# Cached stick-breaking keys loaded into the ring's key tiles and turned by VectorE, and cross-attention's key tiles requested a step ahead

## The chip, the cores and the metric

The kernel runs on one core of a Trainium2 chip. TensorE (PE), VectorE (DVE), ScalarE (ACT) and GpSimd (POOL) each run their instructions in order and wait for each other by semaphores; SyncE (SP) issues all of the kernel's DMAs here, also in order. The metric is the time of one execution in microseconds on the device; lower is better. The time before is 1880.95 us, the median of three runs (1879.8, 1880.95, 1893.64).

## The reference

One step of a hybrid encoder: 1024 prompt rows of one stream and 16 new rows of each of 8 running streams, 1152 rows in all, width 1024, fp32. The parts that the change touches are the attention of the 8 running streams over cached keys, and the cross-attention of these streams over cached memory:

```python
def mixers(u, p, past):
    proj = jnp.einsum('bnd,de->bne', u, p['w_in'])
    sq, sk, sv, fq, fk, fv, fg, z, xbc, dt = split_last(proj, IN_SIZES)
    ...
        sb_k = jnp.concatenate([past['sb_k'].astype(sk.dtype), sk], axis=1)
        sb_v = jnp.concatenate([past['sb_v'].astype(sv.dtype), sv], axis=1)
        sb_o = sb_attend(sq, sb_k, sb_v, qpos, kpos)
    ...
def sb_attend(q, k, v, q_pos, k_pos):
    z = jnp.einsum('bqhd,bkhd->bhqk', q, k).astype(jnp.float32) * (HEAD_DIM ** -0.5)
    valid = k_pos[None, :] < q_pos[:, None]
    log_keep = jnp.where(valid, jax.nn.log_sigmoid(-z), 0.0)
    after = lax.cumsum(log_keep, axis=3, reverse=True) - log_keep
    w = jnp.where(valid, jnp.exp(jax.nn.log_sigmoid(z) + after), 0.0)
    return jnp.einsum('bhqk,bkhd->bqhd', w, v.astype(jnp.float32)).astype(q.dtype)

def cross_attend(u, mk, mv, wq, wo):
    q = jnp.einsum('bnd,de->bne', u, wq).reshape(b, n, X_HEADS, X_HEAD_DIM)
    s = jnp.einsum('bnhd,bmhd->bhnm', q, mk.astype(q.dtype)).astype(jnp.float32) * (X_HEAD_DIM ** -0.5)
    pr = jax.nn.softmax(s, axis=-1)
    o = jnp.einsum('bhnm,bmhd->bnhd', pr, mv.astype(jnp.float32)).astype(u.dtype)
    return jnp.einsum('bne,ed->bnd', o.reshape(b, n, D_MODEL), wo)
```

The cached stick-breaking keys are 8 streams x 1024 positions x 4 heads x 64 (8.4 MB), the cached memory keys 8 streams x 256 positions x 4 heads x 256 (8.4 MB). Beside these the layer has a FoX attention with the same cache layout, an SSD scan, the projections and a SwiGLU feed-forward.

## The kernel before

Products in fp32 precision are made as three reduced-precision products of split operands (`mm3`, L338 to L340): every weight is loaded raw, copied to a high part (ACT) and subtracted to a low part (POOL). A *ring* of buffers holds them: four raw tiles (tag `wr`, `raw_t`, 128x528) and three pairs of split tiles (tags `wh` and `wl`, 128x1056). `w_unit` (L313 on; its load is L324) fills them for one unit of a projection.

The program runs in stages: memory projection and norms (to about 75 us), the projection `w_in` woven with stick-breaking attention (m = 0), then FoX (m = 1) and the SSD scan (about 150 to 700 us), the output projection, cross-attention (about 805 to 1060), and the feed-forward to the end. `pipeline` takes one unit of attention at a time and after each lets a filler go one step, which is a piece of the projection. The order on each engine is then set by a scheduler from a timeline that it simulates, with priorities (`hp`) that the code gives; the code's order is its start.

**Cached keys of the running streams.** `decode_units(0)` puts four pairs of streams into the attention pipeline, as units 3, 7, 11 and 15 (`AT0`). `rows(p)` makes the scores of a pair in two halves of 512 positions (`emit_past`). Each half needs two key tiles, one a stream, that have head dimension on partitions and positions along the row. `load_k(hf, b2)` makes one: two DMAs of 256 KB bring the keys as they lie (2 KB runs, L892) into two raw tiles of the ring, eight PE transposes turn 128x128 blocks into PSUM (L898), and two ACT copies of 128x512 (L900) bring them into the tile `kf`, which takes a slot of `wh` or `wl`. `quads` (L883) then multiplies 32 columns of queries with 512 positions, four products side by side on PE. A raw tile is free for the next weight load once its transposes are done, and a `kf` once its products are.

For m = 0 that is 16 calls of `load_k`: 32 DMAs, 128 transposes and 32 copies; for FoX (m = 1) the same again, which the change leaves.

**Cross-attention.** For each head, `x_query(hd)` projects the queries of all rows (`psd<-act,wh` on PE, six steps, two pairs of the ring), and `both(hd - 1)` runs the previous head's attention between its steps: `x_prompt` for the prompt rows and `x_sample` for the running streams, two steps of it after each step of the projection (`weave`, L435). In `x_sample` (L1571) a head's cached keys come in four tiles (pool `ws`), each by four DMAs of 32 partitions x 16 runs of 256 B (L1603) and one DVE transpose in blocks of 32x32 in place (L1607). `products` (L1592) multiplies after every second tile. Head 3 has no next projection: its `x_sample` and `x_prompt` run beside `loads()`, which brings the outputs of heads 0 to 2 back (`act<-osc`, L1392; first six blocks of 128x4x384 with heads 0 and 1), and the start of the next projection, `wo_x` (`psd<-wh,act` on PE), which reads them.

## Time and profile before

| | |
|---|---|
| median of 3 runs | 1880.95 us (1879.8 to 1893.64) |
| profiled execution | 1883.03 us, of it 1881.3 in the span |
| busy PE, DVE, ACT, POOL | 97%, 48%, 42%, 33% of the span |
| mean granted PE clock | 0.989 of full speed |
| L898, key transposes of m = 0 (128) | 18.5 us busy on PE |
| L900, copies of them (32) | 17.9 us busy on ACT |
| L1607, DVE transposes of memory keys (16) | 19.9 us busy on DVE |
| DMA | 296.6 MB in 312,028 packets, 113,340 of them under 512 B |

A row of a group names the source line, the engine, the operation, the tile written and the tiles read, the shapes, the count, busy time in us, mean ns of one, and the idle time of the engine just before them with what ended it. In the chain and the timelines the first number is the start in us, the second the length; `SPq` is SP issuing a DMA, and `[2.46 <-DMA act<-osc]` is 2.46 us of idle time that this DMA ended. Matmuls are pipelined, so that their busy times overlap; the price of one is read from the distance of starts or from the chain.

### The profile page before, as it was taken

To read this page: it belongs to the slowest core of one execution; us is meant where nothing else is said; L and a number is where in the kernel's file an instruction comes from. 1 tells how busy PE (TensorE), PEld (TensorE's weight loads), DVE (VectorE), ACT (ScalarE), POOL (GpSimd) and SP (SyncE) were. 2 spreads that over 40 slices of the span, in tenths; PEclk is the share of its full clock that TensorE was granted. 3 is DMA by queue.
4 is the path that set the end of the run, shared out by engine and by line. 5 is a ranking of instruction groups with operands and counts; after the bars stand their busy time and mean duration, and the time that the engine had idled before them with its cause. 6 is when DMAs were issued, how large, how long until landed. Compare 5 with 4: busy or idle time off the path is not lost.

```text
span 1881.3 us, 32105 instructions
## 1 busy us (share of the span) xinstructions
PE 1822.3 (97%) x12008; PEld 1625.2 (86%) x12008; DVE 894.1 (48%) x1798; ACT 793.9 (42%) x1703; POOL 617.3 (33%) x921
## 2 busy tenths in 40 slices
PE   7999999999999989999989989999999999999998
PEld 5899878888967768899968879999999999888886
DVE  3412323475656873454444596333333333455554
ACT  6533543545455862343322464333333333344443
POOL 7622424445216663111111107445444542000000
PEclk9999998999999999999989999999999999999999
DMA  9464654437587882257695124333222223657572
GB/s 338 148 186 153 207 144 134 144 104 209 174 263 252 282 297 92 107 140 175 172 289 188 68 74 116 90 86 77 71 71 71 71 71 93 215 185 246 172 245 88
DMA packets 312028, 296.63 MB, mean 158 GB/s; under 512 B 113340, under 2 KB 263844, under 8 KB 311872
## 3 DMA queue, kind: packets, MB, share of 16 engines
q1 hardware_dynamic: 311872, 294.57, 51.5%
q8 instruction: 95, 1.56, 0.3%
q14 instruction: 61, 0.50, 0.1%
HBM read 225.12 MB, written 69.91 MB: 157 GB/s over the span
## 4 chain that ended last, share of the span: by engine, by line
PE 80%; DMA 6%; issue 4%; POOL 4%; DVE 3%; ACT 2%; SPq 1%; DVEq 0%; POOLq 0%; ACTq 0%
PE psd L1897 11%; PE psd L338 9%; PE psd L339 9%; PE psd L340 9%; PE pst L1897 8%; PE pss L338 4%; PE pss L1897 4%; PE pss L340 4%; PE pss L339 4%; POOL wl L132 2%; PE pso L1897 2%; PE pst L338 2%; PE pst L340 2%; PE pst L339 2%; PE pso L603 1%
## 5 line engine op out<-in xcount | busy, mean ns | idle before, releaser
L132 POOL TENSOR_TENSOR wl<-wr,wh 128x256 fp32r<-128x256 f32 (+2 forms) x152 | 118.0, 809 | 254.2 <-ACT wh L292 190.9
L338 PE MATMUL psd<-act,wh 128*128 128x384 f32 x528 | 181.7, 344 | 0.0
L339 PE MATMUL psd<-act,wh 128*128 128x384 f32 x528 | 181.1, 343 | 0.2 <-DVE act L279 0.2
L340 PE MATMUL psd<-act,wl 128*128 128x384 f32 x528 | 180.2, 342 | 0.6 <-POOL wl L132 0.6
L1897 PE MATMUL pst<-bT,tr 128*128 128x256 f32 (+1 forms) x1068 | 155.0, 293 | 0.0
L1897 PEld LDWEIGHTS pst<-bT,tr 128*128 128x128 f32 x1068 | 144.9, 188 | 0.1
L340 PE MATMUL psd<-wh,act 128*128 128x512 f32 (+3 forms) x424 | 137.5, 326 | 0.1
L339 PE MATMUL psd<-wl,act 128*128 128x256 f32 (+3 forms) x414 | 135.1, 327 | 2.2 <-POOL wl L132 2.2
L338 PE MATMUL psd<-wh,act 128*128 128x256 f32 (+3 forms) x414 | 134.2, 328 | 2.6 <-DMA act<-osc 2.5
L1897 PE MATMUL psd<-bT,tr 128*128 128x320 f32 (+1 forms) x912 | 132.9, 295 | 0.6 <-POOL tr L132 0.6
L1897 PEld LDWEIGHTS psd<-bT,tr 128*128 128x128 f32 x912 | 124.7, 188 | 1.0 <-POOL tr L132 0.9
L132 POOL TENSOR_TENSOR tr<-u,tr 128x256 fp32r<-128x256 f32 x110 | 82.4, 778 | 101.8 <-ACT tr L1733 83.9
L253 POOL TENSOR_SCALAR sm<-sm 128x1 f32<-128x1 f32 (+2 forms) x27 | 8.7, 322 | 298.9 <-ACT y L2008 208.9
L1872 DVE TENSOR_TENSOR tr<-tr,pst 128x256 f32<-128x256 f32 (+1 forms) x86 | 38.6, 449 | 139.8 <-ACT tr L1869 106.5
L132 POOL TENSOR_TENSOR ws<-ws 128x256 f32<-128x256 f32 (+2 forms) x100 | 71.0, 738 | 98.4 <-DVE ws L532 84.7
L340 PEld LDWEIGHTS psd<-act,wl 128*128 128x128 f32 x528 | 99.2, 188 | 3.1 <-issue 1.9
L339 PEld LDWEIGHTS psd<-act,wh 128*128 128x128 f32 x528 | 99.3, 188 | 2.4 <-issue 1.5
L338 PEld LDWEIGHTS psd<-act,wh 128*128 128x128 f32 x528 | 99.4, 188 | 2.1 <-issue 1.8
L132 POOL TENSOR_TENSOR tr<-raw,tr 128x256 fp32r<-128x256 f32 x94 | 69.2, 764 | 83.6 <-ACT tr L1733 75.4
L1733 ACT CAST tr<-u 128x512 fp32r<-128x512 f32 x130 | 76.5, 620 | 28.9 <-PE pst L1897 5.9
L338 PEld LDWEIGHTS psd<-wh,act 128*128 128x128 f32 x414 | 79.7, 193 | 10.3 <-DMA act<-osc 2.7
L340 PEld LDWEIGHTS psd<-wh,act 128*128 128x128 f32 x424 | 81.5, 192 | 8.2 <-issue 2.1
(642 smaller groups left out, 4645.5 us busy)
## 6 DMA issues: line engine op xcount, KB each, us to landing
u<-w_down SPq DMA_DIRECT2D x40, 512.0 KB
raw<-w_down SPq DMA_DIRECT2D x26, 512.0 KB
st<-qksc SPq DMA_DIRECT2D x48, 256.0 KB
wr<-w_in SPq DMA_DIRECT2D x44, 256.0 KB
tr<-hidsc SPq DMA_DIRECT2D x55, 192.0 KB
hidsc<-tr SPq DMA_DIRECT2D x34, 288.0 KB
qksc<-sg SPq DMA_DIRECT2D x48, 192.0 KB
wr<-cache_sb_k SPq DMA_DIRECT2D x32, 256.0 KB
```

Of the source, the lines that this page charges most:

```text
L132: POOL.tensor_tensor(out=out[:, a0:a1], in0=in0[:, a0:a1], in1=in1[:, a0:a1], op=op)
L253: POOL.tensor_scalar(v, ss, inv, EPS, ALU.mult, ALU.add)
L338: PE.matmul(out, ah, bh, start=start, stop=False)
L339: PE.matmul(out, ah, bl, start=False, stop=False)
L340: PE.matmul(out, al, bh, start=False, stop=stop)
L603: return PE.matmul(po[r:r + 64, q_], vt[:, 2 * (k0 + i) + j, :], pfs[i][:, sl], start=start and k0 == 0 and (j == 0 or qp > 0), stop=k0 + ...
L1733: ACT.copy(hi, src)
L1872: DVE.tensor_tensor(out=at(out, g), in0=at(x, g), in1=ps[g][:, :GW[g]], op=op)
L1897: PE.matmul(dst[g][:, :GW[g]], x[:, ka], y[:, k, :], start=start and k == 0 and m == 0, stop=stop and k == 3 and m == 2, skip_group_check= ...
```

## The change

For m = 0, `load_k` now brings the keys straight into the `kf` tile, by four DMAs of 32 partitions x 32 runs of 128 B each (L891 of the new file), so that each 32x32 block holds 32 positions of one half of a head. One DVE transpose turns the blocks in place (L892). `quads` reads the tile by a view whose neighbouring positions are 64 elements (256 B) apart. The 32 loads of 256 KB become 64 of 128 KB; 128 PE transposes and 32 ACT copies go, 16 DVE transposes of 128x1024 come. No raw tile is taken for keys, and a `kf` tile is held from its load on. FoX's keys go the old way.

In cross-attention the load and the transpose of a tile are helpers of their own (`x_keys`, `turn`). For heads 0 to 2 each tile's load is asked for one step before its transpose. Head 3's four tiles are loaded and turned during its own query projection: two at its first step, in the ring's third pair, and two at its fourth, in `ws`.

```diff
+            def load_k(hf, b2):
+                if m == 0:
+                    kf = ring.tile([P, 1056], F32, tag=("wh", "wl")[b2], name="kf")[:, :1024]
+                    src = ck[2 * p + b2, hf * 512:(hf + 1) * 512, :].rearrange("(i t) (n g j) -> g i (t n) j", t=16, n=2, g=4)
+                    for g in range(4):
+                        SP.dma_start(out=kf[32 * g:32 * g + 32].rearrange("i (b j) -> i b j", j=32), in_=src[g])
+                    DVE.transpose(kf, kf)
+                    return kf.rearrange("c (t n i) -> c n i t", t=16, n=2)
...
-                return kf
+                return kf[:, :1024].rearrange("c (n i t) -> c n i t", n=2, t=16)
...
-                    quads(ps, lambda b2, nb: kf[b2][:, nb * 512:(nb + 1) * 512])
+                    quads(ps, lambda b2, nb: kf[b2][:, nb])
...
+    def x_keys(hd, k, home=None):
+
+        raw = (home or ws_t)()[:, :1024]
+        for g in range(4):
+            SP.dma_start(out=raw[32 * g:32 * g + 32].rearrange("i (t c) -> i t c", c=64),
+                         in_=cmk[k * 512:k * 512 + 512, hd * 256 + 64 * g:hd * 256 + 64 * g + 64]
+                         .rearrange("(i t) c -> i t c", t=16))
+        return raw
...
+        kfs = keys or [x_keys(hd, 0)]
+        for k in range(4):
+            if not keys and k < 3:
+                kfs.append(x_keys(hd, k + 1))
+            if not keys:
+                turn(kfs[k])
+            if k % 2:
+                two = [by_rows(t) for t in kfs[k - 1:k + 1]]
+                products(ps, k // 2, lambda i, x: two[i // 2][:, x, :, i % 2 * 16:i % 2 * 16 + 16])
+            yield
...
-        weave(x_query(hd, q), att, 2, "xa")
+        keys = []
+        for n, _ in enumerate(x_query(hd, q)):
+            if hd == 3 and n in (0, 3):
+                for k in range(2):
+                    keys.append(x_keys(3, len(keys), None if n else
+                                       lambda k=k: ring.tile([P, 1056], F32, tag=("wh", "wl")[k], name="kf")))
+                    turn(keys[-1])
+            for _ in range(2):
+                with hp("xa"):
+                    next(att, None)
...
-    smp, prm, ld = x_sample(3, q), x_prompt(3, q), loads()
+    smp, prm, ld = x_sample(3, q, keys), x_prompt(3, q), loads()
```

The order moves with it. On SP, before, near the keys of the second pair of streams (the hole at 262 to 290 us): three key loads, then weights of the projection (`wr<-w_in`), the cached values (`vr`) and the convolution state.

```order
L892 DMA wr<-cache_sb_k 128x512 x3
L324 DMA wr<-w_in 128x2x256
L324 DMA wr<-w_in 128x2x8
L324 DMA wr<-w_in 128x2x256
L324 DMA wr<-w_in 128x2x8
L324 DMA wr<-w_in 128x2x256
L670 DMA p_fox_logf<-lf 128x8x4
L671 DMA s_fox_logf<-lf 128x4
L324 DMA wr<-w_in 128x2x8
L324 DMA wr<-w_in 128x2x256
L324 DMA wr<-w_in 128x2x8
L952 DMA vr<-cache_sb_v 128x1024
```

After, the same pair's keys on SP: the first eight loads, with weight loads ahead of and behind them.

```order
L324 DMA wr<-w_in 128x2x256
L324 DMA wr<-w_in 128x2x8
L324 DMA wr<-w_in 128x2x256
L324 DMA wr<-w_in 128x2x8
L891 DMA kf<-cache_sb_k 32x32x32 x4
L976 DMA mixsc<-so 128x2x32
L891 DMA kf<-cache_sb_k 32x32x32 x4
L517 DMA st<-qksc 64x1024
L518 DMA st<-qksc 64x1024
L324 DMA wr<-w_in 128x2x256
L324 DMA wr<-w_in 128x2x8
L324 DMA wr<-w_in 128x2x256
```

The weights no longer follow the key loads that wait for PE, and a group of key loads is eight issues in place of four.

On DVE, before, at the softplus of SSD's step sizes (L415 to L423, on the tile `sg`, 8 values a row), which stands beside the third pair of streams:

```order
L418 TENSOR_TENSOR sg<-sg 128x72
L419 TENSOR_SCALAR sg<-sg 128x72
L421 SCALAR_TENSOR_TENSOR sg<-sg 128x72
L483 COPY sg<-pst 128x384
L421 SCALAR_TENSOR_TENSOR sg<-sg 128x72 x6
L422 SCALAR_TENSOR_TENSOR sg<-sg 128x72
L423 TENSOR_SCALAR sg<-sg 128x72
L818 SCALAR_TENSOR_TENSOR dts<-dts,sg 128x72
```

After, at the same place, the turns of that pair's four key tiles stand between them:

```order
L418 TENSOR_TENSOR sg<-sg 128x72
L892 STREAM_TRANSPOSE kf<-kf 128x1024
L419 TENSOR_SCALAR sg<-sg 128x72
L483 COPY sg<-pst 128x384
L421 SCALAR_TENSOR_TENSOR sg<-sg 128x72 x2
L892 STREAM_TRANSPOSE kf<-kf 128x1024
L421 SCALAR_TENSOR_TENSOR sg<-sg 128x72 x5
L422 SCALAR_TENSOR_TENSOR sg<-sg 128x72
L423 TENSOR_SCALAR sg<-sg 128x72
L818 SCALAR_TENSOR_TENSOR dts<-dts,sg 128x72
L892 STREAM_TRANSPOSE kf<-kf 128x1024 x2
```

Four turns have come in, so that a load that is late holds the softplus and the copy of `pst` (projected keys of FoX) behind it.

On SP, before, where head 3 begins: the first block of the outputs (`act<-osc`) is asked for, then eight loads of head 3's keys (`ws<-cache_mem_k`), and then the next three blocks.

```order
L1392 DMA act<-osc 128x4x384
L1527 DMA osc<-pt 128x2x256 x2
L1603 DMA ws<-cache_mem_k 32x16x64
L1497 DMA sg<-mksc 128x2x256
L1497 DMA sg<-mvsc 128x2x256
L1603 DMA ws<-cache_mem_k 32x16x64 x5
L1527 DMA osc<-pt 128x2x256
L1603 DMA ws<-cache_mem_k 32x16x64
L1527 DMA osc<-pt 128x2x256
L1603 DMA ws<-cache_mem_k 32x16x64
L1392 DMA act<-osc 128x4x384 x3
```

After, at the end of head 3's projection:

```order
L1582 DMA ws<-cache_mem_k 32x16x64 x5
L1606 DMA ws<-cache_mem_v 128x2x256 x4
L1582 DMA ws<-cache_mem_k 32x16x64 x3
L1534 DMA osc<-pt 128x2x256 x2
L324 DMA wr<-wo_x 128x512
L1684 DMA st<-hsc 128x1024 x2
L1399 DMA act<-osc 128x4x384 x6
L1684 DMA st<-hsc 128x1024 x2
L1534 DMA osc<-pt 128x2x256 x2
L1504 DMA sg<-mksc 128x2x256
L1504 DMA sg<-mvsc 128x2x256
```

The last key loads of head 3 are now ahead of all blocks, and the six blocks are asked for in a row.

More of the change, by code (lines that the diff above doesn't have):

```diff
@@ L1569, in x_prompt, with turn, by_rows, x_sample @@
         yield
-    def x_sample(hd, q):
+    def x_keys(hd, k, home=None):
[5 more added lines that the diff above has]
+        return raw
+    def turn(raw):
+        blocks = raw.rearrange("p (t j x) -> p t x j", x=2, j=32)
+        DVE.transpose(blocks, blocks)
+    def by_rows(raw):
+        return raw.rearrange("p (t i x) -> p x t i", x=2, i=32)
+    def x_sample(hd, q, keys=None):
         qs = q[2]
@@ L1596, in x_sample @@
         ps = pS()
-        for e in range(2):
-            kfs = []
-            for i0 in (0, 2):
-                raw = ws_t()[:, :1024]
-                k0 = (4 * e + i0) * 256
-                for g in range(4):
-                    SP.dma_start(out=raw[32 * g:32 * g + 32].rearrange("i (t c) -> i t c", c=64),
-                                 in_=cmk[k0:k0 + 512, hd * 256 + 64 * g:hd * 256 + 64 * g + 64]
-                                 .rearrange("(i t) c -> i t c", t=16))
-                blocks = raw.rearrange("p (t j x) -> p t x j", x=2, j=32)
-                DVE.transpose(blocks, blocks)
-                kfs.append(raw.rearrange("p (t i x) -> p x t i", x=2, i=32))
-                if i0:
-                    products(ps, e, lambda i, x: kfs[i // 2][:, x, :, i % 2 * 16:i % 2 * 16 + 16])
-                yield
+        kfs = keys or [x_keys(hd, 0)]
[8 more added lines that the diff above has]
+            yield
         pr = x_softmax(ps[:, :256].rearrange("p (i m) -> p i m", i=1), 1, sg_t(), 16)
```

4 lines of the change are left out of this document (2 added, 2 removed).

## The prediction

> **What bounds the kernel now.** I read the page first, then the busy time by windows over the two places that the change touches, then the chain of waits and the timelines inside them.
>
> ```profile
> span 1881.3 us, 32105 instructions
> PE 1822.3 (97%) x12008; PEld 1625.2 (86%) x12008; DVE 894.1 (48%) x1798; ACT 793.9 (42%) x1703; POOL 617.3 (33%) x921
> PE 80%; DMA 6%; issue 4%; POOL 4%; DVE 3%; ACT 2%; SPq 1%; DVEq 0%; POOLq 0%; ACTq 0%
> ```
>
> TensorE is busy for 97% of the span and makes 80% of the chain. So work taken from PE shortens the kernel if nothing else becomes late, and work taken from ScalarE or put on VectorE (42% and 48% busy) counts only where PE waits for it. The profiled execution took 1883.0 us, 1.7 us of it outside its span; the median of the runs is 1880.95, 2 us less.
>
> ```profile
> 190.00:450.00 260.00, 247.83 (x1845) 215.27 (x1844) 118.98 (x197) 122.37 (x283) 112.04 (x168) 0.97 0.54 155
> 262.00:290.00 28.00, 23.09 (x147) 16.66 (x146) 13.72 (x44) 16.69 (x37) 14.05 (x19) 0.82 0.79 199
> 955.00:980.00 25.00, 17.83 (x117) 12.13 (x110) 8.32 (x16) 4.75 (x13) 3.65 (x7) 0.80 1.10 316
> 850.00:900.00 50.00, 50.00 (x363) 47.54 (x362) 22.66 (x50) 16.95 (x49) 6.27 (x10) 1.00 0.71 168
> ```
>
> The columns after the length are busy PE, PEld, DVE, ACT and POOL, then the granted clock, the share of the DMA engines and GB/s. The first row is the stretch in which the cached stick-breaking keys are read: PE idles 260 − 247.8 = 12.2 us, 4.9 of them in the hole of the second row. The third row is where cross-attention's head 3 begins: 7.2 us idle of 25. The last row is from heads 0 to 2: PE never waits there. In both holes the clock is lower (0.82, 0.80), so a hole costs more than its idle time.
>
> **Stick-breaking keys: what goes.** Before, each key tile is turned by PE and copied out of PSUM by ScalarE.
>
> ```profile
> L898 PE MATMUL pst<-ident,wr 128*128 128x128 f32 x128 | 18.5, 279 | 2.7 <-DMA wr<-cache_sb_k 2.4 <-ACT kf L900 0.2
> L900 ACT COPY kf<-pst 128x512 f32<-128x512 f32 x32 | 17.9, 596 | 9.7 <-PE pst L898 9.5
> 338.70 0.87 PE pst L898 x8
> 202.77 0.99 PE pss L883 x8
> ```
>
> The transposes overlap, so the chain gives the price: eight take 0.87 us, 0.109 each, and 128 x 0.109 = **−13.9 us** of PE. The 17.9 us of ScalarE are off the path. I count the 2.4 us of waiting with the hole, below.
>
> **What the strided read costs.** The scores of one half of a pair are eight products in 0.99 us; eight such groups make 7.9 us. Afterwards their moving operand steps 256 B from element to element, which no row shows. The nearest rows are these:
>
> ```profile
> 885.85 1.98 PE pss L1592 x31
> 855.04 1.86 PE pss L1592 x32
> L588 PEld LDWEIGHTS pst<-ident,ws x288: 137/141/369, 156.5 to 680.7; 128*128 128x128 f32 x144
> L934 PEld LDWEIGHTS pst<-ident,ws x72: 138/212/231, 221.2 to 686.8; 128*128 128x128 f32 x72
> ```
>
> L1592 with keys (8 B apart) takes 1.98 us, with values (contiguous) 1.86: 6%, or +0.5 us here. A weight load with elements 16 B apart takes 212 ns where a contiguous one takes 141: +50%, or +4 us. I take **+4**, since 16 B is the wider of the two strides; ends +0.5 and +8.5 (the second rival). A gain is excluded: the products are the same.
>
> **What the new loads cost.** A tile now comes in four loads of 1024 runs of 128 B, in place of two with 2 KB runs, and VectorE turns it.
>
> ```profile
> 806.24 13.24 SPq L1603 DMA_DIRECT2D ws<-cache_mem_k  x16
> L1607 DVE STREAM_TRANSPOSE ws<-ws x16: 1235/1246/1250, 812.5 to 972.5; 128x1024 f32<-128x1024 f32 x16
> 944.97 0.34 PE L339 MATMUL psd<-act,wh 128*128 128x384 f32 x1
> 945.15 0.34 PE L340 MATMUL psd<-act,wl 128*128 128x384 f32 x1
> ```
>
> Sixteen cross-attention loads of 512 runs of 256 B take 13.24 us one behind the other: 0.83 us each, 1.62 ns a run. If bytes count, a load of the new kind (also 128 KB) takes 0.83 us; if runs count, 1.65. The two tiles of a group are eight loads: 6.6 to 13.2 us, then two turns of 1.25 us. All 64 loads come to 53 to 106 us of a 260 us stretch whose DMA share is 0.54.
>
> In the Trainium skill, "DMA: Bandwidth & Descriptors" (Specifications) puts the least transfer for full rate at 512 B, with a read-modify-write below. That speaks against the change; the rows bear it out for 256 B (16 x 128 KB in 13.24 us is 158 GB/s, half of the 316 in the hole at 955). By 128 B at half of that again a group would take the 13.2 us.
>
> The cover: a key tile sits in one of three pairs of weight buffers, and the pair before it is used by a projection unit of 72 products that start 0.18 us apart (the last two rows), 12.6 us. So the load is hidden if it starts one unit ahead, nearly whole even by runs. But the 16 turns (16 x 1.25 = 20 us of VectorE, against 119 us busy there) are queued in order: a turn that waits for a late load holds the splits and scans behind it, and PE waits for these. I take 1 us for each of the eight groups, **+8**; ends 0 and +42 (the third rival).
>
> **What goes with the old loads.** The raw key tiles shared four buffers with the weights of the projection, and were freed only by PE's transposes.
>
> ```profile
> 267.75 1.35 SPq L892 DMA_DIRECT2D wr<-cache_sb_k  x3
> 269.19 4.07 SPq L324 DMA_DIRECT2D wr<-w_in  x5
> 271.21 1.65 PE L898 MATMUL pst<-ident,wr 128*128 128x128 f32 x9 [2.24 <-DMA wr<-cache_sb_k]
> 279.79 7.79 DMA xc<-state_conv
> ```
>
> In the hole at 262 to 290, keys and weights are requested at once, PE waits 2.24 us for a key, and the load of the convolution state lands late behind them. In the new order the weights no longer stand behind key loads that wait for PE. The hole costs 4.9 us idle and (1 − 0.82) x 23.1 = 4.2 of clock, 9.1. I take two thirds, **−6**, since state_conv's load keeps its place behind other large ones; ends 0 and −9.
>
> Sum of the first part: −13.9 + 4 + 8 − 6 = **−8**.
>
> **Cross-attention, heads 0 to 2: nothing.** Loads are asked for a step earlier, but PE is 50.00 us busy of 50 in 850 to 900; VectorE's waits for those keys (22.2 us in all, next rows) have no PE behind them except at head 3.
>
> **Head 3.**
>
> ```profile
> DVE ws L1607 <- DMA ws<-cache_mem_k: 22.2, 12, 4.1
> 959.04 6.41 SPq L1603 DMA_DIRECT2D ws<-cache_mem_k  x5
> 968.04 1.83 SPq L1392 DMA_DIRECT2D act<-osc  x3
> 961.68 0.50 PE L338 MATMUL psd<-wh,act 128*128 128x512 f32 x1 [2.46 <-DMA act<-osc]
> 963.15 1.93 PE L1592 MATMUL pss<-ws 128*32 128x256 f32 x16
> 968.20 0.39 PE L338 MATMUL pss<-kt,st 128*128 128x256 f32 x1 [0.68 <-ACT kt L1505]
> 973.76 2.03 PE L1592 MATMUL pss<-ws 128*32 128x256 f32 x16 [3.28 <-DVE ws L1607]
> 993.59 1.07 PE L1592 MATMUL pss<-ws 128*32 128x256 f32 x16
> 976.32 0.63 PE L338 MATMUL psd<-wh,act 128*128 128x512 f32 x1
> 976.75 0.63 PE L339 MATMUL psd<-wl,act 128*128 128x512 f32 x1
> 980.76 0.40 PE L338 MATMUL psd<-wh,act 128*128 128x512 f32 x1
> 981.00 0.39 PE L339 MATMUL psd<-wl,act 128*128 128x512 f32 x1
> ```
>
> Now the query projection of head 3 has ended, and nothing is left to hide a load. SP first issues the key loads, about 1.3 us apiece (6.41 for five), and only then the output blocks (act<-osc) that the next projection reads; PE waits 2.46 us for the first block, then 3.28 us for the turned keys of head 3, and stands behind them in order. After the change these keys are loaded and turned under the projection, and the six act<-osc loads stand in a row behind fewer others. Of the 7.2 us idle I keep 3 for the first block, which still can be asked for only when the projection's buffers close. The clock: two groups at L1592 take 0.9 us longer than the one at 993.59, and nine products start 0.43 us apart instead of 0.24; together 1.8 + 1.7 = 3.5 us, which go with the idle time. So −4.2 − 3.5, **−8**; ends −3 and −11. The two tiles that sit in the last free weight pair delay the splits of the next weights to the end of the projection; 3 us of the kept idle time cover that too.
>
> **The rivals.** *Both holes close and the loads hide* (faster). For it: a unit of 12.6 us against a group's 6.6 to 13.2. Against it: state_conv. −13.9 + 4 + 0 − 9 − 11 = −30: about 1852.
>
> *The strided read counts by pieces.* L1592's keys pass 31 x 256 elements in 1.98 us, 4.0 an ns, two to a 16 B piece; if two pieces an ns is the limit, a group of 4096 elements 256 B apart takes 2.05 us, not 0.99, and eight cost +8.5: about 1871. For it: the 50% of the weight load. Against it: only 6% at 8 B. The Trainium skill's "SBUF — State Buffer" (Specifications (TRN2)) has such a rule: lines of 16 B, at least two hits a line for full bandwidth. The trace agrees so far as the 8 B row, with two hits, loses little.
>
> *Late keys take the place of the transposes* (slower). Where a key tile gets its buffer less than 13.2 us before its group, and runs set the price, VectorE stands at the turn and PE behind it. With 8 us of cover each of eight groups waits 13.2 − 8 = 5.2 us: +42 in place of +8, so about 1867 + 34 = 1901, more with a lower clock. For it: the DMA share of the stretch would rise from 0.54 x 260 = 140 us by 106, less the old loads (8.4 MB at 316 GB/s, 27 us), to 0.84 of it. Against it: the wait of turns in cross-attention (at most 4.1 us) hardly reached PE.
>
> *Head 3's hole stays*, since the act<-osc loads are what it waits for and the DMA engines are full there (1.10, 316 GB/s): −8 − 2 = −10, about 1873.
>
> **How the numbers follow.** Sum: −8 − 8 = −16; 1883.0 − 16 = **1867 us**. The forecast has a chance of 0.44 (its own range 1857 to 1878), both holes closed 0.20, the read by pieces 0.08, late keys 0.15, head 3 unchanged 0.13. The range 1848 to 1894 leaves out under a tenth at the fast end and the worse two thirds of late keys. One per cent, what a measurement here can tell from no change, is 18.8 us: faster is under 1862.1, slower over 1899.8. Faster: 0.20 and a third of the forecast, 0.34. Slower: most of late keys, 0.12. Within: 0.54.
>
> **What would show it.** Right: no PE transposes in 190 to 450 and PE's busy time some 10 us lower; the eight score groups near 1.5 us each; idle time in 190 to 450 about as before; no wait of PE for a turned key at head 3 and its 25 us window under 4 us idle at a clock near 1. The step on loads is wrong if VectorE's waits at the new turns exceed some 20 us with PE waits behind them, or if a group of eight loads takes over 14 us to land. The forecast as a whole is wrong if PE's idle time in the first stretch grows by over 20 us, or if the read costs more than doubling.

## The result, and the profile after

The changed kernel takes 1902.47 us (median of 4 runs, 1899.45 to 1903.69); the kernel before, run beside it, 1880.47 (1879.8 to 1893.64). The ratio is 1.0097, with a 95% interval of 1.0073 to 1.0122: the change makes the kernel about 1% slower. The prediction was 1867 us, range 1848 to 1894. It had the wrong sign, and the time lies outside its range.

The profiled execution took 1902.42 us. First its page:

```profile
span 1900.4 us, 31881 instructions
PE 1825.9 (96%) x11880; PEld 1615.5 (85%) x11880; DVE 918.5 (48%) x1814; ACT 778.2 (41%) x1671; POOL 618.0 (33%) x921
```

PE has 128 instructions less and is busy for 3.6 us *more* (1825.9 against 1822.3); the other 15.5 us of the longer span are idle time.

To find the place, I compared the start of the same instructions (same tiles, same operation, same count) in the two traces. How much later the changed kernel is, by the time in the kernel before (median over 20 us, worked out from the two traces). Each such table sets one execution against one, and executions of the same kernel differ: those of the kernel before ran from 1878.97 to 1896.31 us, so that one or two us mean nothing here.

```
at us            120    480    720    880   1100   1860
later by us      0.3    9.5   10.4   10.5   18.9   19.1
```

So 9 us are lost in the stick-breaking stretch, 1 in FoX and 8 at cross-attention's head 3: nearly all where the two parts of the change lie. The windows of the changed kernel over these places (columns as in the prediction):

```profile
190.00:450.00 260.00, 241.83 (x1674) 197.99 (x1673) 131.73 (x204) 101.28 (x241) 104.36 (x162) 0.95 0.58 142
262.00:300.00 38.00, 26.99 (x159) 19.93 (x155) 24.62 (x50) 17.23 (x40) 24.15 (x41) 0.77 0.44 111
280.00:290.00 10.00, 1.93 (x5) 1.33 (x5) 9.86 (x22) 2.27 (x5) 9.95 (x19) 0.64 0.27 62
290.00:300.00 10.00, 8.13 (x38) 6.51 (x39) 5.85 (x16) 2.29 (x5) 3.48 (x6) 0.50 0.29 32
955.00:1060.00 105.00, 89.54 (x525) 74.04 (x524) 39.37 (x91) 28.31 (x80) 17.69 (x27) 0.90 0.61 208
```

and two of the kernel before that were not shown:

```profile
262.00:300.00 38.00, 33.09 (x246) 26.39 (x245) 15.97 (x47) 18.70 (x42) 20.98 (x32) 0.82 0.62 157
955.00:1060.00 105.00, 97.71 (x534) 77.75 (x527) 43.25 (x89) 25.17 (x70) 16.24 (x25) 0.95 0.62 197
```

The idle time of the first stretch rose from 12.2 to 18.2 us although PE had less to do; the old hole did not close but grew (38 us with 11.0 idle, against 4.9), and the granted clock behind it fell to 0.50. Around head 3 the idle time doubled, 7.3 to 15.5 us.

**Stick-breaking.** The score products and the turns of the changed kernel, by line (least, median and largest ns of one; first and last start; shapes). The last row is VectorE's idle time before the turns, in us and times, that loads of keys ended:

```profile
L883 PE MATMUL pss<-kf,st x64: 1265/1292/1321, 185.9 to 439.4; 128*32 128x512 f32 x64
```

```profile
L892 DVE STREAM_TRANSPOSE kf<-kf x16: 1218/1245/1247, 174.9 to 433.7; 128x1024 f32<-128x1024 f32 x16
  DMA kf<-cache_sb_k: 23.8, 13
```

The same row of the kernel before:

```profile
L883 PE MATMUL pss<-kf,st x64: 592/605/617, 198.0 to 432.7; 128*32 128x512 f32 x64
```

The first score group of the changed kernel in PE's timeline:

```profile
185.88 2.40 PE L883 MATMUL pss<-kf,st 128*32 128x512 f32 x8
188.21 0.44 PE L338 MATMUL psd<-act,wh 128*128 128x384 f32 x1
```

A group of eight products holds PE for 188.21 − 185.88 = 2.33 us, where it was 0.99. That is 1.34 more, eight times: 10.7 us. The turns waited 23.8 us for loads, at most 3.2 at once, a little above the bound of 20 that the prediction set. The first two tiles show what a group of eight loads takes (SP's and VectorE's timelines):

```profile
167.37 1.39 SPq L891 DMA_DIRECT2D kf<-cache_sb_k  x2
174.89 1.25 DVE L892 STREAM_TRANSPOSE kf<-kf 128x1024 f32<-128x1024 f32 x1 [2.38 <-DMA kf<-cache_sb_k]
178.81 1.25 DVE L892 STREAM_TRANSPOSE kf<-kf 128x1024 f32<-128x1024 f32 x1 [2.67 <-DMA kf<-cache_sb_k]
```

From the first issue to the second turn, which waited for a load, are 11.4 us, with four stores (`qksc<-sg`) issued between the eight loads and the DMA engines full (a share of 0.99 from 167.4 to 178.8): between the 6.6 and 13.2 of the prediction, nearer to the price by runs.

PE's timeline in the hole (the last column is the idle time before, and what ended it):

```profile
279.63 0.22 PE L573 MATMUL pss<-mask_sb,identr 128*128 128x128 f32 x1
284.88 0.79 PE L570 MATMUL pss<-st 128*128 128x512 f32 x1 [5.03 <-ACT ws L530]
...
288.85 0.60 PE L692 MATMUL psd<-lf,sg 128*128 128x32 f32 x2 [2.64 <-DVE lf L668]
290.85 0.63 PE L693 MATMUL psd<-so,sg 128*128 128x28 f32 x2 [1.40 <-DVE so L690]
...
298.39 0.59 PE L338 MATMUL psd<-wh,act 128*128 128x264 f32 x1 [0.39 <-DVE fnew L736]
```

None of these waits ends at a key. They end at the sigmoids of the prompt's stick-breaking scores on ScalarE (L530), which free the scores' buffers, and at the chain of small steps that makes FoX's gates (L668 to L736), while VectorE and GpSimd are full: 9.86 and 9.95 us of the 10 from 280. VectorE's timeline shows what became of that chain. Its first part, 29 small steps that make the logarithms of the gates and their sums (first step L415, last L690), before and after:

```profile
267.41 0.18 DVE L415 TENSOR_SCALAR sg<-sg 128x36 f32<-128x36 f32 x1 [0.93 <-ACT sg L414]
272.30 1.15 DVE L690 TENSOR_TENSOR so<-so,lf 128x4 f32<-128x4 f32 x6
```

```profile
276.70 0.32 DVE L415 TENSOR_SCALAR sg<-sg 128x36 f32<-128x36 f32 x1
280.11 2.73 DVE L532 TENSOR_TENSOR_SCAN ws<-ws 128x1024 f32<-128x1024 f32 x1
289.87 0.93 DVE L690 TENSOR_TENSOR so<-so,lf 128x4 f32<-128x4 f32 x5
```

Before, these steps take 6.0 us. After, they take 14.1: three scans of the prompt's stick-breaking rows (L532, 4.3 us in all) stand between them, and the steps themselves are busy for 10.2 us in place of 5.8, while GpSimd is busy for 13.6 of the 14.1 us (before, not at all). What makes the steps longer, no run tests.

**Head 3.** PE's timeline, ScalarE's and SP's:

```profile
968.77 1.04 PE L1616 MATMUL pss<-ws 128*32 128x256 f32 x16
982.47 0.68 PE L338 MATMUL psd<-wh,act 128*128 128x512 f32 x1 [2.77 <-DVE st L1339]
1001.31 0.58 PE L338 MATMUL pss<-kt,st 128*128 128x256 f32 x1 [10.65 <-ACT pt L1491]
```

```profile
983.63 0.59 ACT L1557 CAST pt<-pst 128x512 fp32r<-128x512 f32 x1 [10.11 <-DMA osc<-pt]
1000.24 0.47 ACT L1491 ACTIVATE pt<-pss,sm 128x256 f32<-128x256 f32 x1 [4.63 <-DMA osc<-pt]
```

```profile
962.36 7.59 SPq L1399 DMA_DIRECT2D act<-osc  x6
972.85 1.91 SPq L1534 DMA_DIRECT2D osc<-pt  x2
```

Head 3's key groups (L1616) now start without a wait; the old 3.28 us wait for a turned key is gone. In its place PE stands 10.65 us for ScalarE, which waits for a buffer of `pt`, a pool of four buffers of 128x512 that softmax weights and outputs of cross-attention share. The buffers hold head 2's outputs, and are free only when their stores (`osc<-pt`) have landed; these are issued behind six output blocks of 786 KB each. The pair issued from 972.85 on had its data at 966.55, at the end of VectorE's last subtraction: it stood over 6 us behind the blocks and two residual loads (`st<-hsc`). ScalarE's wait ends some 10 us after this issue, at 983.63, in a time in which the DMA engines are full (window of the changed kernel):

```profile
965.00:990.00 25.00, 22.23 (x154) 16.74 (x147) 6.54 (x13) 4.90 (x14) 2.75 (x6) 0.93 1.06 373
```

The next pair has its data at 973.97 and is issued at 988.81, behind head 3's own small loads, eight loads of cached values and three of weights.

In the kernel before the waits for such stores were short (its waits from 940 to 1010):

```profile
ACT pt L1550 <- DMA osc<-pt: 2.8, 1, 2.8
ACT pt L462 <- DMA osc<-pt: 1.0, 1, 1.0
```

### The profile page after: what moved, and what is told of

The parts are those of the page before. It is cut to its first block, busy times and chain, and to the rows that moved or that the text cites. A ratio compares the mean times of both kernels' runs of the same rounds, so it can differ in the third digit from the quotient of the medians.

```text
span 1900.4 us, 31881 instructions
## 1 busy us (share of the span) xinstructions
PE 1825.9 (96%) x11880; PEld 1615.5 (85%) x11880; DVE 918.5 (48%) x1814; ACT 778.2 (41%) x1671; POOL 618.0 (33%) x921
## 5 line engine op out<-in xcount | busy, mean ns | idle before, releaser
L132 POOL TENSOR_TENSOR wl<-wr,wh 128x256 fp32r<-128x256 f32 (+2 forms) x152 | 112.7, 774 | 257.2 <-ACT wh L292 218.1
L132 POOL TENSOR_TENSOR ws<-ws 128x256 f32<-128x256 f32 (+2 forms) x100 | 77.9, 807 | 107.5 <-DVE ws L532 95.5
L338 PEld LDWEIGHTS psd<-wh,act 128*128 128x128 f32 x414 | 79.8, 193 | 14.7 <-issue 3.3
L339 PEld LDWEIGHTS psd<-wl,act 128*128 128x128 f32 x414 | 79.7, 193 | 11.7 <-issue 4.0
L1761 ACT CAST tr<-u 128x512 fp32r<-128x512 f32 x130 | 76.5, 620 | 28.9 <-PE pst L1925 5.9
```

The source lines that it names most:

```text
L132: POOL.tensor_tensor(out=out[:, a0:a1], in0=in0[:, a0:a1], in1=in1[:, a0:a1], op=op)
L338: PE.matmul(out, ah, bh, start=start, stop=False)
L339: PE.matmul(out, ah, bl, start=False, stop=False)
L1761: ACT.copy(hi, src)
```

## The experiments

Ratios are to the kernel before on the same chip, with 95% intervals. "Later at 480" and so on are taken from the traces as in the table above.

**1 and 2: the parts alone.** One kernel with the stick-breaking part of the change alone, one with the cross-attention part alone, each with its half of the change's diff word for word. In short:

```diff
+                    for g in range(4):
+                        SP.dma_start(out=kf[32 * g:32 * g + 32].rearrange("i (b j) -> i b j", j=32), in_=src[g])
+                    DVE.transpose(kf, kf)
```

```diff
+    def x_sample(hd, q, keys=None):
...
-    smp, prm, ld = x_sample(3, q), x_prompt(3, q), loads()
+    smp, prm, ld = x_sample(3, q, keys), x_prompt(3, q), loads()
```

> Only the stick-breaking part of the change; cross-attention as before. Theory, from the two traces: the same work starts 9.5 us later from 460 us on, so this part alone makes the kernel slower: about 1880.5 + 9.5 = 1890 us, with each group of eight products at L883 at 2.3 us (8 x 1.35 = +10.8 us) and a hole near 280 to 296 us. Rival: the delay comes from the two parts together (cross-attention's loads are far off, so this would be a surprise): then about 1872 us as forecast for this part.

> Only the cross-attention part; stick-breaking keys as before. Theory: at head 3 the same work starts 8 us later in the changed kernel, so this part alone gives about 1880.5 + 8 = 1888 us, with an idle time of PE of about 10 us behind the softmax of head 3's prompt rows (L1491) and the hole of 7 us before gone. Rival: the old forecast of -8 us, 1872 us.

Stick-breaking alone: 1894.03 us, ratio 1.0049 (1.0034 to 1.0065), 10.0 us later at 480 and 10.2 at the end. Cross-attention alone: 1892.05, ratio 1.0041 (1.0026 to 1.0056), 0.5 us later at 880 and 8.5 at 1100. Together that is 0.9%, nearly the whole loss: the parts add up, and each loses by itself. In the second kernel the new wait is there too (PE's timeline):

```profile
992.42 0.58 PE L338 MATMUL pss<-kt,st 128*128 128x256 f32 x1 [12.42 <-ACT pt L1484]
```

**3: read the keys in stored order.** The first kernel, but each product takes its positions in the order in which they lie after the turn: 32 neighbouring elements in a row, then a step to the next block.

```diff
-                return kf.rearrange("c (t n i) -> c n i t", t=16, n=2)
+                return kf.rearrange("c (t n i) -> c n t i", t=16, n=2)
```

> Like the stick-breaking part alone, but the score products read the turned tile in the order in which it lies (32 positions in a row) instead of every 64th element. The loads, the turns and the order of all instructions are the same; the positions of the scores are permuted, so that the sample's stick-breaking output is another. Theory: the read at a stride of 256 B is what the products pay, 1.35 us a group of eight; the groups come down from 2.33 to about 1.0 us and the kernel by 8 x 1.35 = 10.8 us against the stick-breaking part alone, to about 1879. Rival: the products are long for another reason (tile freshly written by VectorE, or the four products at one tile): the groups stay at 2.3 us and the time at 1890.

```profile
L883 PE MATMUL pss<-kf,st x64: 590/593/617, 188.5 to 431.6; 128*32 128x512 f32 x64
```

1888.39 us, ratio 1.0008 (0.9991 to 1.0025). The products are back at 593 ns, in rows of 32 as good as the contiguous read of before. It is 2.9 us later at 480, of which 1.9 were there at 120, before the part begins: 1.0, against 10.2 with the strided read. So the read costs about 9 us of the part's 10, a little less than the 10.7 by the groups. It leaves the part near the kernel before, without the gain that the transposes should have brought.

**4: long runs.** The first kernel with the read as it was in the change, but each load brings 32 runs of 4 KB, whole rows of four positions.

```diff
-                    src = ck[2 * p + b2, hf * 512:(hf + 1) * 512, :].rearrange("(i t) (n g j) -> g i (t n) j", t=16, n=2, g=4)
+                    src = ck[2 * p + b2, hf * 512:(hf + 1) * 512, :].rearrange("(g i r) c -> g i (r c)", g=4, r=4)
```

> Like the stick-breaking part alone, strided read included, but each of the 64 key loads brings 32 runs of 4 KB instead of 1024 of 128 B (the same bytes; the keys in the tile are then not those of the positions, so that the sample's stick-breaking output is another). Theory: the short runs are not what costs; VectorE waits less at the turns (23.8 us before), but PE hardly: within 3 us of the stick-breaking part alone, about 1888. Rival: late keys are what makes the hole and the other delays: 8 to 13 us less, 1877 to 1882.

1888.06 us, ratio 1.0014 (0.9999 to 1.0028); 4.1 us later at 480, against 10.0 with the short runs. The turns still waited, but less (VectorE's idle time before the turns, us and times):

```profile
  DMA kf<-cache_sb_k: 19.3, 11
```

The short runs are worth about 6 us of the part's time, between the two theories. No kernel had both the long runs and the fast read of experiment 3.

**5: the output blocks behind head 3's keys and values.** The cross-attention part alone, with four of the six first output blocks asked for only after head 3's own small loads (`mksc`, `mvsc`).

```diff
+            mem_ins[hd] = SP.dma_start(out=t, in_=src[:, hd * 256:(hd + 1) * 256].rearrange("(m p) c -> p m c", p=P))
...
-            load_chunk(first[c], o_sc, c, 0)
+            with tc.issue_after(mem_ins[3].ins) if c >= 1 else nullcontext():
+                load_chunk(first[c], o_sc, c, 0)
```

> The cross-attention part alone, with one order forced: of the six blocks of earlier heads' outputs (act<-osc), only the first two may be requested before head 3's memory keys and values of the prompt (sg<-mksc, sg<-mvsc), the other four after. Theory: six blocks in a row (4.7 MB) ahead of the stores of head 2 and of these loads make the pt buffers late, and so the stall of 12.4 us at the scores of head 3's prompt rows; with four blocks moved behind, that stall shrinks by at least 6 us, and the kernel comes to 1880 to 1884 us, at most 3 us slower than before. Rival: the stall comes from head 3's score products standing earlier (or from the tiles that they hold), not from the blocks: then it stays over 10 us and the time at about 1889 to 1892.

1894.48 us, ratio 1.0062 (1.0046 to 1.0079); 10.6 us later at the end, not better than the 8.1 without it. PE's longest wait there fell from 12.4 to 6.7 us, and the projection then waited for the blocks (5.1 us in four waits, none without the edit), while the waits for stores stayed:

```profile
ACT pt L462 <- DMA osc<-pt: 11.8, 1, 11.8
DVE pt L463 <- DMA osc<-pt: 11.2, 1, 11.2
PE pss L338 <- ACT pt L1484: 8.0, 2, 6.7
```

My theory that the place of the blocks in SP's queue is the cause, fell in this form.

**6: no key transposes.** The kernel before, without the 128 transposes and the 32 copies: the products read the raw tiles as they are loaded. This is the gain that the change is after, with the old loads. It is not the transposes quite alone: a group's four raw tiles are all that the ring has, and they are now held until the products have read them, where each was free after its own transposes.

```diff
+                if m == 0:
+                    return rvs
...
-                    quads(ps, lambda b2, nb: kf[b2][:, nb * 512:(nb + 1) * 512])
+                    quads(ps, (lambda b2, nb: kf[b2][nb].rearrange("p k c -> p (k c)")) if m == 0 else
+                          lambda b2, nb: kf[b2][:, nb * 512:(nb + 1) * 512])
```

> The kernel before without the 128 transposes and 32 copies of the stick-breaking keys: the score products read the raw tiles as they were loaded (the sample's stick-breaking output is then another); loads, their runs and buffers as before. It measures the first term of the prediction by itself. Theory that the transposes are all on the path: -13.9 us, about 1867. Rival theory, from the stretch at 265 to 290 us, which is as long with transposes in it as without: those of the second pair run while PE waits for the chain of FoX's gates, and cost nothing: -5 to -10 us, 1871 to 1876, with the stretch from the last product of 260 columns to the first of 264 columns still about 25 us.

1896.21 us (1889.67 to 1902.06), ratio 1.0079 (1.0047 to 1.011): slower. Its four executions lie in two pairs, near 1890.6 and 1901.5. In the profiled one, the fastest (1889.67), it is 4.4 us later at 720 than at 120. The windows of this kernel and of the kernel before, and this kernel's PE timeline:

```profile
150.00:470.00 320.00, 291.08 (x2094) 256.73 (x2096) 148.17 (x232) 129.35 (x300) 140.69 (x204) 0.96 0.54 155
```

```profile
150.00:470.00 320.00, 307.83 (x2255) 273.46 (x2254) 140.88 (x234) 145.66 (x335) 137.35 (x209) 0.98 0.54 158
```

```profile
284.49 0.60 PE L692 MATMUL psd<-lf,sg 128*128 128x32 f32 x2 [6.89 <-POOL st L879]
```

Over the whole span PE's busy time fell by 14.2 us (1822.3 to 1808.1); in this window it fell by 16.8, part of it work that now comes after 470, and the idle time rose from 12.2 to 28.9. A hole of 6.89 us stands at the FoX gates, as in the changed kernel, and another 6.0 us end at loads of cached values (`vr<-cache_sb_v`), for which PE did not wait before. So the gain fails to come with the old loads too; how much of that is the raw tiles held longer, no run tells.

VectorE's chain of gate steps is long here as well: 16.0 us from L415 to the end of L690, with four scans between, against 6.0 and none before. The other traces divide in the same way. All kernels that leave out PE's transposes and keep the gates in their place (the changed kernel, experiments 1, 3, 4, 6 and 8) take 14.1 to 16.8 us, with three or four scans between the steps; all that keep the transposes (the kernel before, experiments 2, 5, 7, 9 and 12 to 16) take 6.0 to 6.2, with none.

**7: heads 0 to 2 alone.** The cross-attention part without its head 3 pieces.

```diff
-        for n, _ in enumerate(x_query(hd, q)):
-            if hd == 3 and n in (0, 3):
...
+        weave(x_query(hd, q), att, 2, "xa")
```

> The cross-attention part for heads 0 to 2 alone (each tile's load one step ahead); head 3 as before. Theory: PE never waited there, so nothing comes of it by 950 us (within 1 us of before), and at head 3 the order moves only a little: within 3 us of before. Rival: the earlier requests alone already move the queue at head 3, and the loss of 8 us is there with head 3's own keys loaded late.

1889.63 us, ratio 1.0043 (1.0022 to 1.0063); 2.4 us later at 880, of which 1.5 were there at 120, and 6.0 at 1100. The earlier requests of heads 0 to 2 change little at heads 0 to 2, but they move what stands at head 3, which loses 3.6 us, and where ScalarE again waits for the stores (one wait of 12.1 us in its trace). PE stands only 3.5 us for ScalarE's `pt` there, and 5.0 for output blocks. So ScalarE's wait is not made by the head 3 pieces alone.

**8: another layout for the same edit.** Stick-breaking alone, with each group of 32 partitions loaded so that 32 neighbouring positions stand in a row, in the right order for the read of experiment 3: eight loads of 512 runs a tile in place of four of 1024, runs of 128 B as before.

```diff
+                    src = ck[2 * p + b2, hf * 512:(hf + 1) * 512, :].rearrange("(t i) (n g j) -> g n i t j", t=16, n=2, g=4)
                     for g in range(4):
+                        for n in range(2):
+                            SP.dma_start(out=kf[32 * g:32 * g + 32].rearrange("i (t n j) -> i n t j", t=16, n=2)[:, n], in_=src[g, n])
```

> The stick-breaking part alone with the positions laid out so that the products read 32 neighbouring positions in a row and all outputs are right; the price is eight loads of 512 runs of 128 B for a tile in place of four of 1024. Theory: like the contiguous read before it, groups of 1.0 us and about 9 us less than the stick-breaking part alone, 1881 to 1885; 64 more issues on SP cost little. [...]

1887.58 us, ratio 1.0015 (0.9998 to 1.0033). The products take 593 ns here, and it is still no better than the kernel before; the turns waited 37.9 us for loads, against 23.8. No version of the stick-breaking part that does all its work came closer.

**9, 10 and 11: FoX's gates woven into the next projection.** If the hole at 280 comes from the chain of gate steps, spreading these (`fox_sums`) between the steps of the projection behind them should fill it. Three kernels: the kernel before with this edit, experiment 6 with it, experiment 8 with it.

```diff
-        yield from fox_sums()
+        gates = fox_sums()
+        next(gates)
...
-                yield from z_proj(int(o[1]))
+                for _ in z_proj(int(o[1])):
+                    next(gates, None)
+                    yield
+                drain(gates)
```

> The kernel before with one change of order: the sums of FoX's gates (the chain from L692 to L735) are woven between the steps of the next projection unit (128x264) instead of standing ahead of it. Theory: the stretch from the last product of 260 columns to the first of 264 is as long as that chain, 24.5 us, whatever PE has to do in it, and PE idles there for 4.9 us at a lower clock; woven, the hole and its clock go: 5 to 9 us less, 1872 to 1876. Rival: PE's work there is what takes the time: no change, 1880.

> The same weaving on the kernel without the 128 transposes and 32 copies (score products read the raw tiles, so that the sample's stick-breaking output is another). Theory: without the fixed stretch, PE's work counts again, and the transposes are worth 8 to 14 us: 1860 to 1868, that much below the woven kernel with transposes, where without the weaving they were worth nothing. Rival: the loss without transposes was spread over many small waits of a changed order: then still within 3 us of the woven kernel with transposes.

> The same weaving on the stick-breaking part with eight loads a tile and products that read neighbours (all outputs right). Theory: against the same kernel without weaving (about 7 us over before in its middle) 8 to 12 us less, so 1872 to 1878, faster than both kernels; the short runs keep it above the kernel without transposes. Rival: late keys hold VectorE also here, 1880 or more.

All three are slower: 1892.47 us, ratio 1.0041 (1.0019 to 1.0063); 1893.7, 1.0042 (1.0022 to 1.0063); 1903.03, 1.0082 (1.0057 to 1.0107).

```
later by us, at        120    740   1860
before, woven          0.9    7.8    8.1
no transposes, woven   0.3    2.5    5.4
eight loads, woven     0.4   14.3   13.4
```

Between 200 and 700 us these kernels run the same instructions in another order, some 18 us earlier and others as much later, so that the first time at which a comparison means anything is behind FoX, at 740. The theory that weaving pays, fell: it costs 7 us in the kernel before and 9 with eight loads (13.9 later from 120 to 740, against 4.7 unwoven), and saves 2 without transposes (2.2 against 4.4). No theory of mine gives these signs.

**12: no stores of head 2.** The cross-attention part alone, leaving out the stores of head 2's outputs and making head 1's twice in their stead, before head 3 begins.

```diff
-        for x, src in enumerate((hi, lo)):
-            SP.dma_start(out=f32(o_sc[2 * hd:2 * hd + 2, x, :, c0:c0 + n]).rearrange("k p t -> p k t"),
+        for to in {0: (0,), 1: (1, 2)}.get(hd, ()):
+            for x, src in enumerate((hi, lo)):
+                SP.dma_start(out=f32(o_sc[2 * to:2 * to + 2, x, :, c0:c0 + n]).rearrange("k p t -> p k t"),
...
```

> The cross-attention part alone, without the stores of head 2's outputs in the window where head 3 begins (head 1's stores are made twice in their place, earlier; the outputs are then not right). Theory: at head 3 the softmax waits for one of four pt buffers, which stores of head 2 hold until they have landed behind 4.7 MB of reads; without these stores the waits for osc stores (10.4 + 4.9 + 4.9 us before) go, PE's idle time from 940 to 1030 falls from 18.4 us to under 9, and the loss of 8 us is gone: 1880 or less. Rival: the reads of output blocks and residual rows are what PE waits for: the idle time stays over 14 us.

The windows of experiment 2 and of this kernel around head 3, and this kernel's waits there:

```profile
940.00:1030.00 90.00, 71.64 (x472) 60.26 (x471) 34.63 (x86) 27.11 (x77) 14.71 (x22) 0.92 0.76 248
```

```profile
940.00:1030.00 90.00, 80.57 (x528) 66.56 (x527) 38.51 (x96) 29.03 (x84) 17.55 (x26) 0.94 0.71 229
```

```profile
PE pss L338 <- ACT pt L1484: 3.9, 3, 2.1
```

PE's idle time fell from 18.4 to 9.4 us, its wait for `pt` from 13.7 in all (12.4 at once) to 3.9, and in this window no wait for a store is left, although eight blocks are asked for in a row. Head 3 now adds 2.1 us (5.3 later at 1100, 3.2 at 880) where it added 8.0. So in these traces the stores that hold `pt` cause some 6 of the 8 us that head 3 loses. The whole kernel hardly shows it: 1891.34 (1886.06 to 1896.98), ratio 1.0031 (1.001 to 1.0053), 0.7 us under experiment 2 by the medians. The profiled execution, 1887.98, is one of its faster ones. Between 120 and 880, where the edit changes nothing, it falls 2.1 us behind and experiment 2 0.7: so much differs between executions.

**13: every key transpose twice.** The kernel before, with 128 transposes more: the price of this PE work from the other side.

```diff
-                            PE.transpose(tp[:, (2 * nb + k) * P:(2 * nb + k + 1) * P], rvs[q][:, k, nb * P:(nb + 1) * P],
+                            for _ in range(2 - m):
+                                PE.transpose(tp[:, (2 * nb + k) * P:(2 * nb + k + 1) * P], rvs[q][:, k, nb * P:(nb + 1) * P],
...
```

> The kernel before with each of the 128 key transposes made twice. Theory that PE's work is what the stretch is made of: +13.9 us, about 1895. Theory that part of them runs in holes that chains of other engines leave: less than that, +5 to +10. Theory that the order chosen for the changed costs decides: any value, with idle time of PE at other places than before.

1901.9 us, ratio 1.01 (1.0083 to 1.0117); 16.9 us later at 480, 19 from 600 on. Adding 13.9 us of PE work costs 19; taking the same 13.9 away with the old loads (experiment 6) costs too.

**14, 15 and 16: nothing but the order.** Three kernels with exactly the work of the kernel before, each with one number of its plan changed: the fourth pair of streams one unit of attention earlier (14 for 15 in `AT0`), the first pair one later (4 for 3), and the blocks of cross-attention's head 3 one step later.

```diff
-AT0, AT1 = (3, 7, 11, 15), (4, 8, 12, 16)
+AT0, AT1 = (3, 7, 11, 14), (4, 8, 12, 16)
```

```diff
-AT0, AT1 = (3, 7, 11, 15), (4, 8, 12, 16)
+AT0, AT1 = (4, 7, 11, 15), (4, 8, 12, 16)
```

```diff
-X0, X1, XL = 2, 2, 2
+X0, X1, XL = 2, 3, 2
```

> No work is added, taken away or changed: the fourth pair of streams enters the attention pipeline as unit 14 instead of 15. Theory: the order of before is a favourable one, and a change of order by itself costs 3 to 8 us: 1884 to 1889, lost at 350 to 480 us. Rival: the order as such is worth under 2 us, and what the other kernels lost came from their changed work.

> No work is changed: the first pair of streams enters the attention pipeline as unit 4 instead of 3. Theory that a change of order costs by itself: 3 to 8 us over before, lost at 190 to 300 us. Rival: within 2 us of before.

> No work is changed: at head 3 the loads of output blocks start one step of the attention later in the code's order. Theory that a change of order at head 3 costs by itself: 3 to 8 us over before, lost between 940 and 1020 us, with waits for osc stores over 10 us in sum. Rival: within 2 us of before.

1902.99 us, ratio 1.0112 (1.0096 to 1.0127); 1885.28, 1.0008 (0.9997 to 1.002); 1884.94, 1.0003 (0.9994 to 1.0013).

```
later by us, at         120    340    740   1860
pair 4 one earlier      1.7    2.1   24.6   24.2
pair 1 one later        1.3    5.4    3.5    3.5
blocks one step later   0.5    1.0    0.0    0.1
```

Of the three, only the first is slower than the kernel before by its executions; the theory of 3 to 8 us for any new order held for none of them. But a plan with no work changed can cost as much as the whole change does: 18 us by the medians, and over 20 in the profiled execution, which was its slowest (1907.26).

## Why the prediction was wrong, point by point

**The transposes (−13.9) brought no gain in any kernel that was run.** The price of the work was right: PE's busy time fell by 14.2 us in experiment 6. The step that failed is "work taken from PE shortens the kernel if nothing else becomes late", which rested on a share of 97%. In the stretch from 150 to 470 other chains end nearly as late as PE's. One can be shown. The last product of FoX's value projection (128x260) and the first of the next projection (128x264) bracket the chain of FoX's gates. PE's timeline of the kernel before:

```profile
264.89 0.28 PE L340 MATMUL psd<-wh,act 128*128 128x260 f32 x1
265.01 1.47 PE L898 MATMUL pst<-ident,wr 128*128 128x128 f32 x12
266.69 0.66 PE L898 MATMUL pst<-ident,wr 128*128 128x128 f32 x4 [0.20 <-ACT kf L900]
267.90 1.07 PE L883 MATMUL pss<-kf,st 128*32 128x512 f32 x8 [0.56 <-ACT kf L900]
...
273.41 0.84 PE L898 MATMUL pst<-ident,wr 128*128 128x128 f32 x3
...
276.26 1.07 PE L883 MATMUL pss<-kf,st 128*32 128x512 f32 x8
...
289.45 0.57 PE L338 MATMUL psd<-wh,act 128*128 128x264 f32 x1
```

and of the changed kernel (its other end, 298.39, stands above):

```profile
272.63 0.28 PE L340 MATMUL psd<-wh,act 128*128 128x260 f32 x1
```

Before, 28 transposes (nine of them in the row at 271.21 that the prediction shows) and two score groups stood inside these 24.6 us and filled PE while it waited for the gates. After, they are not there, and the bracket is 25.8 us long; without transposes, with the old loads, it is 28.6 (experiment 6):

```profile
266.11 0.28 PE L340 MATMUL psd<-wh,act 128*128 128x260 f32 x1
294.71 0.59 PE L338 MATMUL psd<-wh,act 128*128 128x264 f32 x1
```

So in this stretch taking the transposes away gains nothing, and what is left in their place is idle time at a lower clock. The chain of gates that sets its length did not stay as it was: in the kernels without the transposes the prompt's scans fall between its steps on VectorE, and its first part grows from 6.0 to 14.1 us (16.0 in experiment 6). The prediction looked at VectorE only for the new turns; what it did not see is that the prompt's scans now come earlier in VectorE's order (the one of 1152 elements starts at 269.76, before at 280.23), and that PE waits for what they hold up. No run kept the old order on VectorE without the transposes, so that what this alone costs is not measured.

That covers 28 of 128. For the other 100 only the sum is shown: no kernel without the 128 is faster than before, and adding 128 costs 19 us. Experiment 14 says why no simple sum can hold here: with the same work, another order alone is worth 18 us by the medians, and the scheduler makes a new order when any cost changes. How much of the missing gain is the chain of gates, other chains, the raw tiles held in experiment 6, or a worse order from the scheduler, stays open: experiments 9 to 11 were to tell these apart and did not. That the gain cannot be had is not shown either. If the effects of experiments 3 and 4 (9 and 6 us) add up, long runs with a fast read would leave the part some 5 us faster than before (an estimate: 10 − 9 − 6); nobody ran that.

**The strided read (+4, ends +0.5 and +8.5) was mis-sized.** It is +10.7 by the groups, about +9 in time. The choice of the weight load at 16 B as the nearest row was the error: at 256 B the products take 1292 ns, with 32 neighbours in a row 593. By the prediction's own sign, a read that costs more than doubling (2.33 against 0.99), the forecast as a whole had failed here. The rival by pieces was right: it said 2.05 us a group, 2.33 were measured, 4096 elements at 1.76 an ns. The Trainium skill's "SBUF — State Buffer" (Specifications (TRN2)), with its lines of 16 B and two hits a line for full bandwidth, points the same way as these rows. The rival's total of 1871 failed with the other terms, not with this one.

**The new loads (+8) were about right, as far as they were measured.** Short runs cost some 6 us (experiment 4), and a group lands in 11.4 us. What the 16 turns cost beside the waits was not measured. The price of 0.83 us a load was the distance of SP's issues (the row at 806.24), not of transfers: in that stretch the DMA engines were busy for 0.68 to 0.83 of their share and moved 133 to 140 GB/s, not 158. "Late keys" came out at the right number, 1901, by luck, for the most part by other ways: no PE wait ends at a turned key, and the turns waited 23.8 us in all, not 5.2 us of PE in each of eight groups.

**The old hole (−6) grew instead.** I took the wait for a key (2.24 us) and the load of the convolution state for its cause. The key wait did go, and the hole remained, with 11.0 us idle in 38 where there were 4.9. PE's waits in it end at the chain of gates, which had become 8 us longer on VectorE, and at the sigmoids of L530.

The four terms do not add up: 9 for the read and 6 for the runs are 15, and the part lost 10, although experiment 6 lost some 4 in its trace. The remaining 5 to 9 us lie within what an order can do (18 us in experiment 14, nothing clear of noise in 15 and 16). (The sum of the faster rival, −30, gives 1853, not 1852; nothing hangs on it.)

**Heads 0 to 2 (0): right in place, with a catch.** Under 1 us is lost up to the end of those heads (experiments 2 and 7), but their earlier requests alone leave head 3 later (experiment 7).

**Head 3 (−8) came out +8.** The wait for the keys vanished, as the prediction said. The failed step is what would be late next: I kept 3 us for the first output block and looked no further down the queue. I had the six block loads "in a row behind fewer others"; that row, 7.59 us of SP's queue, is also what the next stores of head 2 stand behind, as those after them stand behind head 3's own loads, and these stores hold the four `pt` buffers that head 3's softmax needs. Before, the waits for them came to 3.8 us from 940 on. Experiment 12 shows that the held buffers make most of the loss. Experiment 5 shows that moving the blocks behind small loads is no cure. That the blocks' bytes delay the stores, beside their place in the queue, is argued, not shown: it fits DMA engines that are full (1.06) while the stores are on their way, and no run left out the bytes alone.

## What to carry to other kernels

A share of 97% on one engine does not make its work the price of the kernel: look in the stretch itself at which chain would end next, and test it by leaving the work out before writing the replacement. Where a scheduler sets the order from costs, every edit gives a new order, so compare the starts of the same instructions in both traces, and run an edit that changes the order alone to learn how much of a difference is only that. Where a load moves forward in a queue, list the stores behind it and the buffers which those hold.

## What the runs showed of the hardware

- A moving operand of fp32 elements 256 B apart takes 1292 ns for a product of 128x32 by 128x512, four of them side by side; with 32 neighbouring elements in a row, then a step, 593, and the contiguous one of before 605. In groups of eight that is 2.33 against 0.99 us.
- Eight loads of 1024 runs of 128 B (1.05 MB) took 11.4 us to the turn of the second tile, among four stores and with the DMA engines full (0.99, 198 GB/s); the same bytes in runs of 4 KB shortened the stretch by some 6 us over 64 loads.
- The same 29 small steps on VectorE were busy for 5.8 us while GpSimd stood idle and for 10.2 us while it was busy for 13.6 of 14.1 us. What lengthened them is not tested.
- The granted clock falls behind idle time and stays low for a while: in the changed kernel it was 0.64 from 280 to 290, where PE was busy for 1.93 us, and still 0.50 from 290 to 300, where it was busy for 8.13.
